# An add and GELU kernel: the first two loads of y take 16 KB and 48 KB per row instead of 32 KB each, into one buffer

## The chip, the cores and the metric

The kernel runs on one core of a Trainium2 chip. The metric is the device time of one execution in microseconds (us), lower is better. Before the change three executions took 120.02, 120.04 and 120.09 us, median 120.04.

## The reference

Two float32 matrices of 1024 x 4096 are added, and the GELU in its tanh form is taken of each element of the sum.

```python
z = x + y
return (0.5 * z * (1 + np.tanh(np.sqrt(2 / np.pi) * (z + 0.044715 * z ** 3)))).astype(np.float32)
```

16 MiB of x and 16 MiB of y are read and 16 MiB are written: 50.33 MB in all.

## The kernel before

Each of the 128 partitions holds eight rows of the matrix, which are 32,768 consecutive elements (128 KB) in memory. One tile z of that width holds x, then the sum, then the result, all in place. The work on it is cut into 16 chunks of 2,048 columns (`CH`). A chunk c passes through four steps:

- add c: z = z + y, on DVE for the chunks 0, 2, 4, 6, 8 and 12 (`by_dve`), on POOL for the other ten (line 149 for both).
- mag c: w = |z| on ACT, into a tile w in PSUM (line 154). There are two buffers of w (`PS = 2`), so mag c also needs end c-2.
- gelu c: w = gelu(-w) on ACT, in place (line 157).
- end c: z = max(z, 0) + w on DVE (line 166). This gives the GELU of z, since gelu(z) = max(z, 0) + gelu(-|z|). Chunk 8 (`FIRST`) does it in two halves.

All transfers are issued by SP, on one queue, in a fixed order: y0, x0, y1, x1, y2, y3, then the three stores. The loads of x have 16,384 columns each (64 KB per partition, 8 MiB), those of y 8,192 each (32 KB per partition, 4 MiB). "Row" below is what one transfer moves for one partition. y lies in a pool of two buffers of 8,192 columns, so y2 takes the buffer of y0 and has to wait for the adds of chunks 0 to 3, and y3 takes that of y1 and waits for the adds of chunks 4 to 7 (lines 129 to 132, and `needs` in lines 183 to 185). The stores have 16,384, 10,240 and 6,144 columns: chunks 0 to 7, 8 to 12 and 13 to 15. Each waits for the ends of its chunks, and store 0 also for the first half of end 8 (lines 137 to 143).

The order of each engine's instructions is written out by hand (lines 173 to 179). POOL takes its adds by rising chunk: 1, 3, 5, 7, 9, 10, 11, 13, 14, 15. ACT takes mag and gelu chunk by chunk. DVE takes add 0, add 2, end 0, end 1, add 4, end 2, end 3, add 6, end 4, end 5, end 6, end 7, add 8, end 8, end 9, add 12, end 10 and the ends after it. An engine works through its list strictly in order: an instruction that waits holds up all behind it. `begin_early` puts the issues of y0 and x0 ahead of the program's opening barrier; `wait_late` rearranges the closing waits. The change doesn't touch either.

Of the kernel before, what the change touches and what calls it, by code (L numbers as in the profile page):

```python
# [8 lines left out]
def begin_early(nc, count):  # L9


    head, body = (b.instructions for b in nc.main_func.blocks[:2])
    SP = mybir.EngineType.SP
    moved = [i for i in body if i.engine == SP and isinstance(i, mybir.InstDMACopy)][:count]
    assert not any(i.sync_info and i.sync_info.on_wait for i in moved)
    assert all(i.regs_accessed() == ((), ()) for i in moved)
    at = next(k for k, i in enumerate(head) if i.engine == SP)
    for k, i in enumerate(moved):
        body.remove(i)
        head.insert(at + k, i)  # L20


def wait_late(nc):

    body, end = (b.instructions for b in nc.main_func.blocks[1:3])
    last = [i for i in body if isinstance(i, mybir.InstDMACopy)][-1]
    (sem,) = [u.id for u in last.sync_info.on_update]
    all_done = end[0]  # L30
    reset = next(i for i in end if isinstance(i, mybir.InstDrain) and i.is_reset_sema)
    at = end.index(reset)
    clear = end[at + 1]
    first, stop = reset.reset_range_start, reset.reset_range_stop
    assert all_done.engine == mybir.EngineType.SP and reset.engine == mybir.EngineType.Pool
    assert isinstance(clear, mybir.InstISA) and clear.engine == mybir.EngineType.Pool
    waits = all_done.sync_info.on_wait
    (its,) = [w for w in waits if w.id == sem]

    end[0] = mybir.InstDrain(  # L40
        name=all_done.name, engine=all_done.engine, debug=all_done.debug, is_reset_sema=False,
        sync_info=mybir.SyncInfo(on_wait=[w for w in waits if w.id != sem], on_update=[]),
    )
    parts = []
    for f, e in ((first, sem), (sem + 1, stop)):
        if f < e:
            nc.gpsimd.sem_clear(range(f, e))
            parts.append(nc.cur_bb.bb.instructions.pop())
    end[at + 1 : at + 2] = parts
    end.append(  # L50
        mybir.InstEventSemaphore(
            name=clear.name, engine=mybir.EngineType.Activation, debug=clear.debug,
            sync_info=mybir.SyncInfo(
                on_wait=[its],
                on_update=[
                    mybir.SyncUpdate(
                        sync_type="semaphore", id=sem, ant_name=its.ant_name,
                        update_mode="sem-sub-imm", update_value=its.wait_value,
                    )
                ],  # L60
            ),
        )
    )


@with_exitstack
def kernel(
    ctx: ExitStack,
    tc: tile.TileContext,
    x: bass.AP,  # L70
    y: bass.AP,
    out: bass.AP,
):

    nc = tc.nc
    P = nc.NUM_PARTITIONS
    fp32 = mybir.dt.float32
    act = mybir.ActivationFunctionType
    alu = mybir.AluOpType

    N, D = x.shape
    assert N % P == 0
    TOT = N // P * D  # L90
    xv, yv, ov = (a.rearrange("(p n) d -> p (n d)", p=P) for a in (x, y, out))

    YS = 8192
    CH = 2048
    PS = 2
    xloads = [16384, 16384]
    yloads = [8192, 8192, 8192, 8192]
    FIRST = 8
    stores = [16384, 10240, 6144]

    def ranges(sizes):
        ends = [sum(sizes[: i + 1]) for i in range(len(sizes))]
        assert ends[-1] == TOT
        return [(e - f, e) for e, f in zip(ends, sizes)]

    xr, yr, sr, cr = (ranges(r) for r in (xloads, yloads, stores, [CH] * (TOT // CH)))
    C = len(cr)

    by_dve = {0: 0, 2: 0, 4: 2, 6: 4, 8: 8, 12: 10}

    def over(rs, lo, hi):
        return [i for i, (a, b) in enumerate(rs) if a < hi and b > lo]

    pool_sb = ctx.enter_context(tc.tile_pool(name="xz", bufs=1))
    pool_y = ctx.enter_context(tc.tile_pool(name="y", bufs=2))
    pool_w = ctx.enter_context(
        tc.tile_pool(name="w", bufs=PS, space=bass.MemoryType.PSUM)
    )

    zt = pool_sb.tile([P, TOT], fp32, tag="z", name="z")  # L120
    yt, wt, ends = {}, {}, {}

    def load_x(i):
        a, b = xr[i]
        nc.sync.dma_start(out=zt[:, a:b], in_=xv[:, a:b])

    def load_y(i):
        a, b = yr[i]
        s, o = divmod(a, YS)
        if o == 0:  # L130
            yt[s] = pool_y.tile([P, YS], fp32, tag="y", name=f"y{s}")
        nc.sync.dma_start(out=yt[s][:, o : o + b - a], in_=yv[:, a:b])  # L132

    def store(i):
        a, b = sr[i]
        ins = nc.sync.dma_start(out=ov[:, a:b], in_=zt[:, a:b])
        if i == 0:
            tc.add_manual_dep(
                ins.ins,
                ends[FIRST].name,  # L140
                mybir.DependencyInfo(mybir.DependencyClass.Sync, mybir.DependencyReason.DATA),
                reason="the stores join the queue when the last load is nearly done",
            )

    def add(c):
        a, b = cr[c]
        s, o = divmod(a, YS)
        eng = nc.vector if c in by_dve else nc.gpsimd
        eng.tensor_add(out=zt[:, a:b], in0=zt[:, a:b], in1=yt[s][:, o : o + b - a])  # L149

    def mag(c):
        a, b = cr[c]
        wt[c] = pool_w.tile([P, CH], fp32, tag="w", name=f"w{c}")
        nc.scalar.activation(out=wt[c], in_=zt[:, a:b], func=act.Abs)  # L154

    def gelu(c):
        nc.scalar.activation(  # L157
            out=wt[c], in_=wt[c], func=act.Gelu_apprx_tanh, scale=-1.0
        )

    def end(c):
        a, b = cr[c]
        parts = 2 if c == FIRST else 1
        n = (b - a) // parts
        for o in range(0, b - a, n):
            ins = nc.vector.scalar_tensor_tensor(  # L166
                out=zt[:, a + o : a + o + n], in0=zt[:, a + o : a + o + n], scalar=0.0,
                in1=wt[c][:, o : o + n], op0=alu.max, op1=alu.add,
            )
            ends.setdefault(c, ins.ins)  # L170


    sp = [(load_y, 0), (load_x, 0), (load_y, 1), (load_x, 1), (load_y, 2), (load_y, 3)]
    sp += [(store, i) for i in range(len(stores))]
    pool = [(add, c) for c in range(C) if c not in by_dve]
    dve, acts = [], []
    for c in range(C):
        dve += [(add, k) for k in sorted(by_dve) if by_dve[k] == c] + [(end, c)]
        acts += [(mag, c), (gelu, c)]

    needs = {
        load_x: lambda i: [],
        load_y: lambda i: [
            (add, c) for c in over(cr, yr[i][0] - 2 * YS, yr[i][1] - 2 * YS)
        ],
        add: lambda c: [(load_x, i) for i in over(xr, *cr[c])]
        + [(load_y, i) for i in over(yr, *cr[c])],
        mag: lambda c: [(add, c)] + ([(end, c - PS)] if c >= PS else []),
        gelu: lambda c: [(mag, c)],
        end: lambda c: [(gelu, c)],  # L190
        store: lambda i: [(end, c) for c in over(cr, *sr[i])] + [(end, FIRST)],
    }
    queues = [sp, pool, acts, dve]
    done = set()
    with tc.manual_schedule():
        one = pool_sb.tile([P, 1], fp32, tag="one", name="one")
        nc.vector.memset(one, 0.0)  # L197
        nc.scalar.activation(out=one, in_=one, func=act.Gelu_apprx_tanh)  # L198
        while any(queues):
            moved = False  # L200
            for q in queues:
                while q and all(n in done for n in needs[q[0][0]](q[0][1])):
                    fn, arg = q.pop(0)
                    fn(arg)
                    done.add((fn, arg))
                    moved = True
                    if q is not sp:
                        break
            assert moved, [q[:1] for q in queues]

    ctx.close()
    tc.close()
    tc.compile()  # L213
    begin_early(nc, 2)
    wait_late(nc)
# [30 lines left out]
```

## Time and profile before

| What | Value |
|---|---|
| Median of three executions | 120.04 us |
| The profiled execution | 120.05 us |
| Its span, from first to last record of the core | 118.6 us |
| Busy: DVE, ACT, POOL | 59.8, 60.8, 55.5 us |
| DMA queue, share of 16 engines | 98.6% |
| First adds start | 31.45 us (DVE), 31.49 us (POOL) |
| Stores issued | 77.61, 96.34 and 107.56 us |

DVE, ACT and POOL are compute engines; SP issues transfers. Times in the views count from the start of the span. Where a line of the profile starts with two numbers they are the start and the duration in us; then come the engine, the line of the kernel, the operation, what it writes and reads with its shape, and how many instructions are merged. What stands in square brackets is how long the engine had been idle before, and what ended that. "SPq" is SP's queue of instructions. "DMA to landing" is the time from a transfer's issue until its data has landed and been signalled.

### The profile page before, as it was taken

What the parts mean: (1) busy time and instruction counts of PE and PEld (TensorE: products, weight loads), DVE (VectorE), ACT (ScalarE), POOL (GpSimd) and SP (SyncE); (2) the same over time, 40 slices, a digit from 0 to 9 for tenths busy, and PEclk for the clock granted to TensorE, in tenths of its full rate; (3) what the DMA queues carried; (4) which work ended last, traced back from release to release, by engine and by line L of the source; (5) the groups of instructions that cost most, each with busy time, mean ns of one, the idle gap of its engine ahead of it and who ended that gap; (6) DMA issues with size and microseconds to landing.
All of it is one profiled execution on the core that took longest, in us unless ns stands there. A gap on an engine that the chain in (4) does not pass through costs nothing.

```text
span 118.6 us, 160 instructions
## 1 busy us (share of the span) xinstructions
DVE 59.8 (50%) x24; ACT 60.8 (51%) x34; POOL 55.5 (47%) x14
## 2 busy tenths in 40 slices
DVE  0000000000399999699994594257999457742000
ACT  5000000000067979999379705797798999940000
POOL 0000000000399999997000029999999999100000
DMA  7989888998889988988899898998899889999996
GB/s 243 464 365 696 354 354 354 663 398 354 354 387 497 531 354 354 707 354 354 354 420 464 365 520 354 531 531 354 354 531 531 354 354 442 442 442 442 398 398 265
DMA packets 1296, 50.33 MB, mean 424 GB/s; under 512 B 144, under 2 KB 144, under 8 KB 144
## 3 DMA queue, kind: packets, MB, share of 16 engines
q1 hardware_dynamic: 1296, 50.33, 98.6%
HBM read 33.55 MB, written 16.78 MB: 424 GB/s over the span
## 4 chain that ended last, share of the span: by engine, by line
DMA 48%; POOL 34%; POOLq 4%; ACT 3%; DVE 2%; issue 0%; SPq 0%; DVEq 0%
POOL z L149 34%; DMA z<-in_x_dram 26%; DMA y<-in_y_dram 21%; POOLq L213 4%; DVE z L166 2%; ACT w L154 2%; ACT w L157 2%; SPq L132 0%; POOLq L149 0%; DVEq L166 0%
## 5 line engine op out<-in xcount | busy, mean ns | idle before, releaser
L149 POOL TENSOR_TENSOR z<-z,y 128x2048 f32<-128x2048 f32 x10 | 55.3, 5563 | 45.6 <-DMA z<-in_x_dram 31.1
L154 ACT ACTIVATE w<-z 128x2048 f32<-128x2048 f32 x16 | 30.1, 1880 | 42.5 <-DVE z L149 36.0
L166 DVE SCALAR_TENSOR_TENSOR z<-z,w 128x2048 f32<-128x2048 f32 (+1 forms) x17 | 36.4, 2157 | 16.0 <-ACT w L157 16.0
L149 DVE TENSOR_TENSOR z<-z,y 128x2048 f32<-128x2048 f32 x6 | 24.0, 4009 | 30.3 <-DMA z<-in_x_dram 30.1
L157 ACT ACTIVATE w<-w 128x2048 f32<-128x2048 f32 x16 | 29.8, 1862 | 0.5
L198 ACT ACT_TABLE_LOAD x1 | 1.3, 1283 | 1.3 <-PEq L230 1.3
L197 DVE MEMSET one<- 128x1 f32 x1 | 0.1, 59 | 1.3 <-PEq L230 1.3
L198 ACT ACTIVATE one<-one 128x1 f32<-128x1 f32 x1 | 0.2, 203 | 0.0
L230 POOL MEMSET const-float32-0.0<- 128x1 f32 x1 | 0.1, 98 | 0.2 <-issue 0.2
L230 POOL MEMSET const-bfloat16-1.0<- 128x1 bf16 x1 | 0.1, 101 | 0.0
L230 POOL MEMSET const-uint8-127<- 128x1 uint8 x1 | 0.1, 101 | 0.0
L230 POOL MEMSET const-float32-1.0<- 128x1 f32 x1 | 0.1, 98 | 0.0
## 6 DMA issues: line engine op xcount, KB each, us to landing
y<-in_y_dram SPq DMA_DIRECT2D x4, 4096.0 KB, 23.7
out_dram<-z SPq DMA_DIRECT2D x1, 5120.0 KB, 14.9
out_dram<-z SPq DMA_DIRECT2D x1, 3072.0 KB, 11.0
z<-in_x_dram SPq DMA_DIRECT2D x2, 44.9
out_dram<-z SPq DMA_DIRECT2D x1, 21.6
```

Source lines behind the costliest of these rows:

```text
L149: eng.tensor_add(out=zt[:, a:b], in0=zt[:, a:b], in1=yt[s][:, o : o + b - a])
L154: nc.scalar.activation(out=wt[c], in_=zt[:, a:b], func=act.Abs)
L157: nc.scalar.activation(out=wt[c], in_=wt[c], func=act.Gelu_apprx_tanh, scale=-1.0)
L166: ins = nc.vector.scalar_tensor_tensor(out=zt[:, a + o : a + o + n], in0=zt[:, a + o : a + o + n], scalar=0.0, in1=wt[c][:, o : o + n], op ...
L197: nc.vector.memset(one, 0.0)
L198: nc.scalar.activation(out=one, in_=one, func=act.Gelu_apprx_tanh)
L213: tc.compile()
L230: nc = _bacc.Bacc("TRN2", target_bir_lowering=False, num_devices=1)
```

## The change

The two buffers of 8,192 columns become one tile of 16,384 columns, which takes as much memory. The first load of y brings 4,096 columns (16 KB per row, 2 MiB) and the second 12,288 (48 KB per row, 6 MiB); the third and fourth stay at 8,192. The order of SP's issues stays. A load of y goes to its column modulo 16,384, so y2 covers the columns of chunks 0 to 3 and y3 those of chunks 4 to 7.

```diff
-    YS = 8192
+    YS = 16384
     CH = 2048
     PS = 2
     xloads = [16384, 16384]
-    yloads = [8192, 8192, 8192, 8192]
+    yloads = [4096, 12288, 8192, 8192]
...
-    pool_y = ctx.enter_context(tc.tile_pool(name="y", bufs=2))
...
-    yt, wt, ends = {}, {}, {}
+    yt = pool_sb.tile([P, YS], fp32, tag="y", name="y")
+    wt, ends = {}, {}
...
     def load_y(i):
         a, b = yr[i]
-        s, o = divmod(a, YS)
-        if o == 0:
-            yt[s] = pool_y.tile([P, YS], fp32, tag="y", name=f"y{s}")
-        nc.sync.dma_start(out=yt[s][:, o : o + b - a], in_=yv[:, a:b])
+        o = a % YS
+        nc.sync.dma_start(out=yt[:, o : o + b - a], in_=yv[:, a:b])
...
-        s, o = divmod(a, YS)
+        o = a % YS
         eng = nc.vector if c in by_dve else nc.gpsimd
-        eng.tensor_add(out=zt[:, a:b], in0=zt[:, a:b], in1=yt[s][:, o : o + b - a])
+        eng.tensor_add(out=zt[:, a:b], in0=zt[:, a:b], in1=yt[:, o : o + b - a])
...
         load_y: lambda i: [
-            (add, c) for c in over(cr, yr[i][0] - 2 * YS, yr[i][1] - 2 * YS)
+            (add, c) for c in over(cr, yr[i][0] - YS, yr[i][1] - YS)
         ],
```

## The prediction

> **What bounds the kernel now.** I read the page's header and DMA rows first, then the time from issue to landing of each tile's transfers, then the instructions in order of time.
>
> ```profile
> span 118.6 us, 160 instructions
> DVE 59.8 (50%) x24; ACT 60.8 (51%) x34; POOL 55.5 (47%) x14
> q1 hardware_dynamic: 1296, 50.33, 98.6%
> ```
>
> No engine is busy for much over half of the span; the one DMA queue is busy for 98.6% of it. The two answers on tiles y and z give when each transfer landed:
>
> ```profile
> DMA to landing us min/median/max: 12.0/23.7/39.8
> DMA to landing us min/median/max: 11.0/21.6/58.8
> ```
>
> Added to the issue times (0.00, 0.43, 1.26, 1.64, 44.68, 57.94, 77.61, 96.34, 107.56) and with the page's row of issues, the landings are y0 12.0, x0 31.35, y1 41.06, x1 60.44, y2 70.14, y3 79.86, store 0 99.2, store 1 111.2, store 2 118.56. Their distances are 19.35 for 8 MiB, 9.71 for 4, 12.0 for 5 and 7.36 for 3: always 2.40 to 2.45 us per MiB, with rows from 24 to 64 KB. So the queue never runs dry, and the row size does not show. Only the first transfer is longer: 12.0 us for 4 MiB, of which 9.7 is stream and 2.3 is the time that a transfer on an idle queue costs beyond its stream (F below).
>
> The queue doesn't run dry because each issue comes early enough. SP's waits and issues:
>
> ```profile
> 44.68 0.33 SPq L132 DMA_DIRECT2D y<-in_y_dram  x1
> 57.94 0.33 SPq L132 DMA_DIRECT2D y<-in_y_dram  x1
> 77.61 0.35 SPq L136 DMA_DIRECT2D out_dram<-z  x1
> 96.34 0.34 SPq L136 DMA_DIRECT2D out_dram<-z  x1
> 107.56 0.33 SPq L136 DMA_DIRECT2D out_dram<-z  x1
> ```
>
> y2 is issued 15.8 us before x1 lands, y3 12.2 us before y2 lands. But store 0 is issued only 2.25 us before y3, the last load, lands; that is F itself, so this issue has next to no slack. Store 0 waits for the first half of end 8, which hangs on DVE's queue:
>
> ```profile
> 33.66 6.59 DVE L149 TENSOR_TENSOR z<-z,y 128x2048 f32<-128x2048 f32 x1
> 52.25 5.62 DVE L149 TENSOR_TENSOR z<-z,y 128x2048 f32<-128x2048 f32 x1
> 67.66 2.29 DVE L166 SCALAR_TENSOR_TENSOR z<-z,w 128x2048 f32<-128x2048 f32 x1 [1.46 <-ACT w L157]
> 70.23 2.29 DVE L149 TENSOR_TENSOR z<-z,y 128x2048 f32<-128x2048 f32 x1 [0.28 <-DMA y<-in_y_dram]
> 31.49 6.61 POOL L149 TENSOR_TENSOR z<-z,y 128x2048 f32<-128x2048 f32 x1 [31.06 <-DMA z<-in_x_dram]
> 51.21 4.51 POOL L149 TENSOR_TENSOR z<-z,y 128x2048 f32<-128x2048 f32 x1
> ```
>
> End 7 ran at 67.66 to 69.95, and add 8 started at 70.23 on the landing of y2: DVE's slack was 0.28 us. The lines also price the adds: 2.28 on DVE and 4.51 on POOL alone, 5.6 to 6.6 where they meet.
>
> **What the Trainium skill says.** "SBUF — State Buffer", in "Who interferes with whom": a DVE instruction with two SBUF inputs contends with a GpSimd instruction that reads SBUF, and the pair of ports is a lock held for the whole instruction. The trace agrees: POOL's add 1, started 0.04 us behind DVE's add 0, took 6.61 = 4.51 + 2.1, and DVE's add 6, started while POOL's add 7 ran (51.21 to 55.72), ended 2.15 after it, at 57.87. The end operation takes w from PSUM and took 2.27 to 2.29 beside POOL. "DMA: Bandwidth & Descriptors", in "Anatomy of one DMA — SWDGE (gpsimd) path", gives a fixed part of about 2.0 us per transfer; this is another path, but the 2.3 here is near it.
>
> **The change part by part.** In the program as built each engine keeps its order of instructions, and SP issues the same nine transfers; only sizes and waits differ.
>
> *Bytes and rows.* The sum of y0 and y1 stays 8 MiB, and each transfer has 128 rows. At 2.42 us per MiB, y1 still lands at 41.06, and x1, y2, y3 as before; only y0 and x0 land earlier, by 2 x 2.42 = 4.84. Cost 0. No row shows 16 or 48 KB; from 24 to 64 KB the price differs by at most 0.05 us per MiB, so for the 8 MiB the bounds are -0.4 and +0.4 us; I take 0.
>
> *Adds 2 and 3 wait for y1.* Before, chunks 0 to 3 were covered by y0. Now y0 holds chunks 0 and 1 alone. On DVE add 2 stands ahead of end 0 and of all behind it, on POOL add 3 ahead of adds 5 and 7. So DVE does add 0 alone, then stops until y1 has landed. I replay the queues with the rows' durations: DVE's next instruction starts 2.20 after the last, ACT's two take 1.88 and 1.86 with starts 1.91 and 1.77 apart (3.68 per chunk), an end starts 0.11 after its gelu, an add 0.09 after a landing.
>
> x0 lands at 31.35 - 4.84 = 26.51. Add 0 26.60 to 28.88, add 1 26.64 to 33.25, gelu 0 done 32.7, gelu 1 done 37.1. Then the wait for y1: add 2 41.16 to 43.44, add 3 on POOL 41.20 to 47.81 (behind add 2's lock). End 0 43.36 to 45.64, end 1 45.56 to 47.84. Add 4 47.76 to 50.04 and POOL's add 5 47.80 to 54.43. ACT: mag 2 needs end 0 (two w buffers): 45.68, gelu 2 done 49.45; gelu 3 51.27 to 53.13; mag 4 53.04, gelu 4 done 56.81; mag 5 56.72, gelu 5 done 60.49. End 2 49.96 to 52.24; end 3 53.24 to 55.53. Add 6 is asked for at 55.44, but POOL's add 7 has held the lock since 54.40, to 58.91; add 6 ends 2.15 later, at 61.06 (before: 57.87). End 4 60.99 to 63.26, end 5 63.19 to 65.46; mag 6 63.30, gelu 6 done 67.07; gelu 7 68.89 to 70.75; end 7 70.86 to 73.15, where it was 67.66 to 69.95: 3.2 us late.
>
> *Add 8 behind end 7.* It is asked for at 73.06. y2 landed at 70.14, and POOL's add 9, which before started 0.04 us behind add 8, starts at 70.27 and holds the lock to 74.78. So add 8 ends at 76.93 (before 72.52). Mag 8 76.97, gelu 8 done 80.74, first half of end 8 80.78 to 82.00; store 0 is issued at 82.02 instead of 77.61: 4.41 late.
>
> *The queue.* y3 lands at 79.86 as before. Store 0 lands F + 8 x 2.42 after its issue: 82.02 + 2.3 + 19.35 = 103.67 against 99.2, +4.47. F of a store on a queue run dry is not in the trace: from below, its issue of 0.35 and some 0.4 for the landing give 82.02 + 0.75 + 19.35 = 102.12, +2.9; from above the 2.3 of the first transfer, +4.5. With the skill's 2.0 it is +4.2. I take +4.3, between the last two.
>
> *Later stores.* DVE's add 12 is asked for at 86.7, behind POOL's add 13 (85.76 to 90.27), ends 92.4, and end 12 ends at 100.83 (before 96.31). Store 1 is issued at 100.86; it keeps the queue fed if this is before 82.02 + 19.35 = 101.37 (F on both sides cancels): 0.5 us of cover. Without it the excess would add to the end one to one. End 15 ends at 111.9, store 2 is due at 101.37 + 12.0 = 113.4: cover 1.5.
>
> *The refills.* y2 now waits for add 3 at 47.81: issued 47.9 (44.68), 10.2 us before it would be late at 60.44 - 2.3. y3 waits for add 6 at 61.06: issued 61.1, 6.7 before 70.14 - 2.3. Both cost 0 under the transfers ahead of them. One buffer in place of two adds no wait: y2's columns are those of adds 0 to 3, y3's of adds 4 to 7.
>
> Sum: span 118.6 + 4.3 = 122.9. This execution took 120.05 with 1.45 outside of the span (the median is 120.04): 124.35.
>
> **The rivals.** *No change, 120.05.* If DVE reached add 6 before POOL takes add 7 at 54.40, add 6 would end near 56.7, mag 6 would start at about 60.4 behind gelu 5, end 7 would end near 70.3, and add 8 would start on y2 as now. For it: chunks 0 and 1 leave ACT early, so only six of eight chunks (22 us) remain at 45.7. Against it: end 3 needs gelu 3 at 53.13, and end 3 would have to end by 54.4, not 55.5; the point from which this decides is 1.1 us.
>
> *The lock is given differently at add 8, 122.7.* If add 8 ran at once at 73.06, it would end at 75.3, and store 0 would be issued at 80.4, 2.8 late, which with the F taken above is +2.65 at the end. Against it: add 6 and add 2 each waited out a whole POOL add.
>
> *Add 8 misses POOL's gap at 74.78, 128.8.* If it were asked for 1.7 us later than worked out, add 10 would hold the lock until 79.3, and all is 4.5 later. Were add 4 to lose the lock to add 5 at 47.8 (they are 0.04 apart), add 6 still ends near 61.2 and add 8 is asked for at about 73.9: inside the gap.
>
> *Faster.* The load path would have to shrink, and no byte leaves it; the 0.4 us bound on rows, with no late store, would be 119.6.
>
> **How the numbers follow.** Forecast 0.81; no change 0.06; lock given at once 0.05; missed gap 0.06; faster 0.02. The forecast's own range is 122.9 to 125.2: F's lower bound (118.6 + 2.9 + 1.45 = 122.95) to F 2.3 with 0.4 for rows or a late store 1. To leave out no more than two in ten the range takes in the lock given at once: 122.6 to 125.4. About 0.2% is what a measurement of this kernel can tell from no change. Slower: 0.81 + 0.05 + 0.06 = 0.92; same 0.06; faster 0.02.
>
> **What would show it.** x0 lands near 26.5 and y1 still near 41; add 2 waits for y; end 7 ends near 73; add 8 takes well over 2.3 us; store 0 is issued near 82, and the DMA row falls in the slices at 80 to 84; the waits of ACT for DVE grow. It is wrong if add 6 ends before 58.5, if store 0 is issued before 78, or if the transfers' pace moves from 2.42 us per MiB.

## The result and the profile after

The changed kernel takes 123.82 us (median of six, 123.76 to 123.90) against 120.11 for the kernel before, measured beside it: a ratio of 1.0309, 95% interval 1.0296 to 1.0323. It is slower by 3.7 us. The forecast was 124.35, in a range of 122.6 to 125.4.

The page of the changed kernel, its header and the rows on DMA (the row of digits is the DMA engines' busy share in 40 slices of 3.06 us):

```profile
span 122.4 us, 161 instructions
DVE 57.8 (47%) x24; ACT 60.4 (49%) x34; POOL 55.5 (45%) x14
DMA  7999779859959897799789897709777979999596
q1 hardware_dynamic: 1296, 50.33, 95.8%
```

The span grew by 3.8 us and no engine is busy for longer; the queue's share fell from 98.6% to 95.8%. The place is the one 0 in the row of digits, the 27th slice, 79.6 to 82.6 us: the queue stood still there. From 79.5 to 82.9 us it moved nothing at all. A table by stretch of time (columns: the stretch, its length, busy time of DVE, ACT and POOL with instructions, clock, share of the DMA engines, GB/s) shows it beside the same stretch of the kernel before; first the changed kernel:

```profile
79.90:83.00 3.10, 2.10 (x2) 3.07 (x3) 3.10 (x2) 1.00 0.05 21
```

and the kernel before:

```profile
79.90:83.00 3.10, 2.20 (x1) 2.40 (x2) 3.10 (x2) 1.00 0.78 338
```

(In so short a stretch the share of the DMA engines is coarse: for 70.0 to 79.9 us the same table gives the kernel before a share of 1.10.)

What ended the gap is SP's issue of store 0. SP's issues in the changed kernel, in order of time (start, duration):

```profile
47.96 0.33 SPq L131 DMA_DIRECT2D y<-in_y_dram  x1
61.22 0.33 SPq L131 DMA_DIRECT2D y<-in_y_dram  x1
82.15 0.35 SPq L135 DMA_DIRECT2D out_dram<-z  x1
100.86 0.34 SPq L135 DMA_DIRECT2D out_dram<-z  x1
111.98 0.33 SPq L135 DMA_DIRECT2D out_dram<-z  x1
```

y2 and y3 are issued 3.3 us later than before, still long ahead of need. Store 0 is issued at 82.15 instead of 77.61, 4.54 us late, after y3 has landed (at about 80.0). The way to it, on DVE and POOL:

```profile
26.79 2.29 DVE L148 TENSOR_TENSOR z<-z,y 128x2048 f32<-128x2048 f32 x1 [25.39 <-DMA z<-in_x_dram]
41.24 2.29 DVE L148 TENSOR_TENSOR z<-z,y 128x2048 f32<-128x2048 f32 x1 [12.16 <-DMA y<-in_y_dram]
47.85 2.29 DVE L148 TENSOR_TENSOR z<-z,y 128x2048 f32<-128x2048 f32 x1
55.53 5.60 DVE L148 TENSOR_TENSOR z<-z,y 128x2048 f32<-128x2048 f32 x1
54.47 4.51 POOL L148 TENSOR_TENSOR z<-z,y 128x2048 f32<-128x2048 f32 x1
70.92 2.29 DVE L165 SCALAR_TENSOR_TENSOR z<-z,w 128x2048 f32<-128x2048 f32 x1 [1.46 <-ACT w L156]
73.13 3.93 DVE L148 TENSOR_TENSOR z<-z,y 128x2048 f32<-128x2048 f32 x1
70.41 4.51 POOL L148 TENSOR_TENSOR z<-z,y 128x2048 f32<-128x2048 f32 x1 [11.42 <-DMA y<-in_y_dram]
```

and add 4 in the kernel before:

```profile
44.57 2.28 DVE L149 TENSOR_TENSOR z<-z,y 128x2048 f32<-128x2048 f32 x1
```

From the top: add 0 starts 4.7 us earlier than before. Add 2 then keeps DVE idle for 12.16 us until y1 has landed, although gelu 0 is done at 32.89 and end 0 could run. Add 4 starts at 47.85, 3.28 us later than before, and this delay is handed on: add 6 is asked for at 55.53 (before 52.25), waits out POOL's add 7 (54.47 to 58.98) and ends at 61.13; end 7 ends at 73.21. Waiting out add 7 is not new: in the kernel before add 6 came behind add 7 by nearly as much (52.25 against 51.21), so it adds nothing to the loss. What is newly lost is the turn at the shared ports that add 8 had ahead of add 9. DVE had 0.28 us to spare there, so add 8 is asked for 2.9 us later than before; POOL's add 9 (70.41 to 74.92) has started by then, add 8 waits it out and takes 1.64 us longer. It ends at 77.06, 4.54 us later than before.

### The profile page after: what moved, and what is told of

Its sections match the earlier page's. It is cut to its first block, busy times and chain, and to the rows that moved or that the text cites. A ratio compares the mean times of both kernels' runs of the same rounds, so it can differ in the third digit from the quotient of the medians.

```text
span 122.4 us, 161 instructions
## 1 busy us (share of the span) xinstructions
DVE 57.8 (47%) x24; ACT 60.4 (49%) x34; POOL 55.5 (45%) x14
## 3 DMA queue, kind: packets, MB, share of 16 engines
q1 hardware_dynamic: 1296, 50.33, 95.8%
## 4 chain that ended last, share of the span: by engine, by line
DMA 33%; ACT 29%; DVE 15%; issue 14%; DVEq 0%
DMA y<-in_y_dram 33%; ACT w L153 18%; ACT w L156 10%; DVE z L165 8%; DVE z L148 7%; DVEq L165 0%
## 5 line engine op out<-in xcount | busy, mean ns | idle before, releaser
L148 DVE TENSOR_TENSOR z<-z,y 128x2048 f32<-128x2048 f32 x6 | 22.1, 3676 | 37.6 <-DMA z<-in_x_dram 25.4
## 6 DMA issues: line engine op xcount, KB each, us to landing
out_dram<-z SPq DMA_DIRECT2D x1, 5120.0 KB, 14.2
out_dram<-z SPq DMA_DIRECT2D x1, 20.8
```

What stands on the lines that cost most here:

```text
L148: eng.tensor_add(out=zt[:, a:b], in0=zt[:, a:b], in1=yt[:, o : o + b - a])
```

## The experiments

The theory, Q: the two loads of y themselves cost nothing. Adds 2 and 3 wait for y1, and add 2 stands at the head of DVE's queue; DVE's and POOL's adds shut each other out; so end 7 and with it end 8 are late, and store 0 is issued only after the queue has run dry. The rivals: R, the rows of 16 and 48 KB or the shared tile cost the time; S, store 0 is the only transfer that is late.

**The shared tile alone.**

```diff
-    yloads = [4096, 12288, 8192, 8192]
+    yloads = [8192, 8192, 8192, 8192]
```

> The one tile for y is kept, but all four loads of y have 8,192 columns (32 KB rows) again. If the loss is store 0 coming late because chunks 2 and 3 wait for y1, nothing is late here: add 2 starts at about 33.7 us, store 0 is issued at 77.6 and the time is 120.1. If the shared tile itself cost something (an added wait of y2 or y3), the time stays near 123.8.

Measured: 120.07 us, ratio to before 1.0002 (0.9991 to 1.0013). One tile in place of two buffers costs nothing; the sizes of the loads are the part that matters.

**A smaller step in the sizes.**

```diff
-    yloads = [4096, 12288, 8192, 8192]
+    yloads = [6144, 10240, 8192, 8192]
```

> In one tile, y0 has 6,144 columns and y1 10,240, so y0 covers chunks 0 to 2 and only add 3, on POOL, waits for y1. By the queues: add 2 is done near 38, ends 0 and 1 before 43, end 7 ends near 67.4, before y2 lands at 70.1, so store 0 is issued near 77.6 and the time is 120.1: a step, not a slope. If unequal rows cost in proportion, about 121.9.

Measured: 120.05 us, ratio 0.9993 (0.9982 to 1.0003). Half of the change costs nothing, so the loss is a step and not in proportion to the rows. Here y0 covers chunks 0 to 2, so that add 2 does not wait for y1. Add 3 on POOL still does; then come end 7 and add 8 of this run:

```profile
41.07 17.63 POOL L148 TENSOR_TENSOR z<-z,y 128x2048 f32<-128x2048 f32 x3 [5.44 <-DMA y<-in_y_dram]
64.88 2.29 DVE L165 SCALAR_TENSOR_TENSOR z<-z,w 128x2048 f32<-128x2048 f32 x1 [1.46 <-ACT w L156]
70.17 2.29 DVE L148 TENSOR_TENSOR z<-z,y 128x2048 f32<-128x2048 f32 x1 [3.01 <-DMA y<-in_y_dram]
```

POOL's wait for y1 alone costs nothing. DVE is done with end 7 at 67.17 and waits 3.01 us for y2: slack where the kernel before had 0.28 us and the changed kernel none.

**Add 2 moved behind end 1, rows of 16 and 48 KB kept.**

```diff
-    by_dve = {0: 0, 2: 0, 4: 2, 6: 4, 8: 8, 12: 10}
+    by_dve = {0: 0, 2: 2, 4: 2, 6: 4, 8: 8, 12: 10}
```

> The changed kernel with one move: on DVE add 2 stands behind end 1 instead of ahead of end 0. If the loss comes from add 2 heading DVE's queue while y1 is on its way, ends 0 and 1 now run before 40 us, add 6 gets the port before add 7, end 7 ends near 69.5, store 0 is issued near 77.6, and the time is 120.1 with rows of 16 and 48 KB. If the rows or the tile cost the time, it stays at 123.8.

Measured: 120.02 us, ratio 0.9992 (0.9979 to 1.0006). DVE and POOL around y1 and at add 6:

```profile
37.08 2.29 DVE L165 SCALAR_TENSOR_TENSOR z<-z,w 128x2048 f32<-128x2048 f32 x1 [2.14 <-ACT w L156]
54.09 2.28 DVE L148 TENSOR_TENSOR z<-z,y 128x2048 f32<-128x2048 f32 x1
54.12 6.63 POOL L148 TENSOR_TENSOR z<-z,y 128x2048 f32<-128x2048 f32 x1
66.92 2.29 DVE L165 SCALAR_TENSOR_TENSOR z<-z,w 128x2048 f32<-128x2048 f32 x1 [1.47 <-ACT w L156]
```

The first line is end 1, done before y1 lands. Add 6 now comes 0.03 us ahead of POOL's add 7, runs in 2.28 us, and it is POOL that waits: the turn that the changed kernel and the kernel before both lost. End 7 ends at 69.21, in time for y2. The loads are those of the changed kernel, so R falls: the place of one instruction in DVE's queue decides over the whole loss.

**A late store 0 alone, on the kernel before.**

```diff
-    FIRST = 8
+    FIRST = 9
```

Store 0 now waits for the first half of end 9 in place of end 8.

> The kernel before, with the loads as they were; FIRST is 9 instead of 8, so store 0 waits for the first half of end 9 and is issued near 82.05 instead of 77.61. If a late store 0 alone is enough, the queue runs dry as in the changed kernel: store 0 lands 20.8 after its issue, at 102.85 instead of 99.2, and the time is 123.7. If the loss is in the loads or the compute, it is 120.1.

Measured: 123.82 us, ratio 1.0307 (1.0282 to 1.0331), the changed kernel's time with the old loads. The issue and, from the page's DMA issues, its time to landing:

```profile
82.01 0.35 SPq L136 DMA_DIRECT2D out_dram<-z  x1
out_dram<-z SPq DMA_DIRECT2D x1, 20.8
```

Stores 1 and 2 are issued at 96.33 and 107.52, as in the kernel before, so here nothing else is late. A store 0 issued at 82 is enough for the whole loss.

**Store 0 freed of end 8, in the changed kernel.** The manual dependence of store 0 is left out, and

```diff
-        store: lambda i: [(end, c) for c in over(cr, *sr[i])] + [(end, FIRST)],
+        store: lambda i: [(end, c) for c in over(cr, *sr[i])],
```

> The changed kernel, but store 0 waits only for the ends of its own chunks 0 to 7 and is issued near 73.2, before y3 lands. If store 0's lateness is the whole loss: 120.1. If all of the later chunks are late with it, store 1 (chunks 8 to 12, 100.86) comes after store 0 has landed at 99.2; it lands 14.2 after its issue at 115.1, store 2 7.4 later at 122.4, and the time is 123.8 as before this edit.

Measured: 123.15 us, ratio 1.0241 (1.0211 to 1.0271). S falls: with store 0 issued at 73.11, 3.0 us of the loss stay, 2.0 of them now ahead of store 1.

```profile
100.75 0.34 SPq L135 DMA_DIRECT2D out_dram<-z  x1
out_dram<-z SPq DMA_DIRECT2D x1, 5120.0 KB, 13.6
out_dram<-z SPq DMA_DIRECT2D x1, 27.1
```

The last line is store 0: it lands at 73.11 + 27.1 = 100.2, 0.5 us before store 1 is issued; store 1 lands at 114.35 and store 2 about 7.3 later. Store 1 took 1.5 us more than the 12.1 that its 5 MiB take in a busy queue at 2.42 us each, so to leave no gap it had to be issued at about 98.7; it came about 2.0 us after that. The expected 123.8 was 0.65 too much because it took for store 1 the 14.2 us of the changed kernel, where it had stood in the queue; on an empty queue it took 13.6. And store 0 ought to have landed at 99.2, not 100.2. That is the other 1.0 us; more on it below.

**Smaller stores, with store 0 waiting as in the change.**

```diff
-    stores = [16384, 10240, 6144]
+    stores = [16384, 4096, 4096, 4096, 4096]
```

> The changed kernel with stores of 16,384 and four times 4,096 columns; store 0 still waits for the first half of end 8. The later stores are then ready well ahead, but store 0 comes at 82.15: the queue has 1.5 us of fixed part and 38.7 us of stream behind that, so about 122.4 of span and 123.8 if the dry queue before store 0 is the loss; 120.1 if the lateness of store 1 or 2 is.

Measured: 124.01 us, ratio 1.0313 (1.0287 to 1.0338). Smaller later stores, the first of them issued at 86.94 in place of 100.86, gain nothing while store 0 is late.

**Both: store 0 freed, and smaller stores.**

> Both edits: store 0 freed of end 8 (issued near 73.2) and four later stores of 4,096 columns. The compute ends as late as in the changed kernel (end 15 near 112), but each store is issued before the queue has worked off the one ahead: ends 9, 11, 13, 15 near 87, 97, 105, 112 against 97.8, 102.6, 107.5, 112.3. Then 120.1. If the late compute itself sets the end: 112 + 1.5 + 4.9 is 118.4 of span, the same; if more stores cost on the queue, or if rows of 16 and 48 KB do, over 121.

Measured: 121.21 us, ratio 1.0079 (1.0055 to 1.0104). Most of the loss is gone, though the compute ends as late as in the changed kernel: the last two stores are issued at 104.57 and 111.93. But 1.1 us stays where nothing was expected to. The queue shows no gap, at 98.8% of a span of 119.8. Store 0 was issued at 73.16 and took 27.1 to land, so at 100.26; less its stream of 19.35 that puts the landing of y3 at 80.9, 1.0 later than in the kernel before. This was new. Store 0 freed alone, without smaller stores, had lost the same 1.0, so the smaller stores were the least likely cause; the store's early issue and the rows were open.

**Store 0 freed in the kernel before**, with the same edit on the old loads and stores.

> The kernel before, loads untouched; store 0 waits only for the ends of chunks 0 to 7 and is issued near 70.0 instead of 77.6, long before y3 has landed. If a store queued behind a running load slows that load, as in the two runs with store 0 freed (y3 landed at 80.85 and 80.89 instead of 79.86), y3 lands near 80.9 here too and the time is 121.1. If the extra 1.0 us there came from the new rows or the smaller stores, it is 120.1.

Measured: 121.24 us, ratio 1.0078 (1.0053 to 1.0103). The page and SP's line:

```profile
69.94 0.35 SPq L136 DMA_DIRECT2D out_dram<-z  x1
out_dram<-z SPq DMA_DIRECT2D x1, 30.4
q1 hardware_dynamic: 1296, 50.33, 98.7%
```

69.94 + 30.4 - 19.35 = 81.0: y3 lands 1.1 late again, with neither new rows nor small stores. It is the early issue. That it is the load which takes longer, and not the store, is read from y3 alone, issued at 57.94 in the kernel before and at 57.90 here; its time to landing there and here:

```profile
DMA to landing us min/median/max: 21.9/21.9/21.9
DMA to landing us min/median/max: 23.1/23.1/23.1
```

**Smaller stores, and store 0 waiting for add 8.** Store 0's manual dependence names add 8 in place of the first half of end 8, and the stores are 16,384 and four times 4,096.

> The changed kernel with stores of 16,384 and four times 4,096 columns, and store 0 waiting for add 8 instead of end 8: issued near 77.1, neither late nor long ahead. If the whole loss is the dry queue, and the 1.1 us left with store 0 freed came from its early issue, y3 lands at 79.9, the queue never runs dry and the time is 120.1, with rows of 16 and 48 KB and all compute from chunk 2 to 15 as late as in the changed kernel. If smaller stores cost the rest, 121.2.

Measured: 120.25 us, ratio 0.9998 (0.9980 to 1.0016).

```profile
76.86 0.35 SPq L135 DMA_DIRECT2D out_dram<-z  x1
111.76 0.33 SPq L135 DMA_DIRECT2D out_dram<-z  x1
q1 hardware_dynamic: 1584, 50.33, 98.8%
```

The span is 118.5. Rows of 16 and 48 KB, the shared tile, the late adds and a compute that ends near 112 are all still there and cost nothing, since store 0 comes neither after y3 nor long ahead of it and each later store in time. None of the versions is faster than the kernel before: where the queue never runs dry and store 0 is not issued long ahead of y3's landing, the span is 118.5 or 118.6.

## Why the prediction was right

**Bytes and rows: 0.** Right. y1 was due to land at 41.06 and add 2 started on it at 41.24; y2, due at 70.14, started add 9 at 70.41. The runs with loads of y in rows of 16, 24, 40 and 48 KB whose store 0 is neither late nor freed of its wait are at 120.0 to 120.3.

**Adds 2 and 3 and the replay of the queues.** Right to about 0.2 us in every step shown here: x0 in use at 26.79 (26.60 forecast), add 6 asked for at 55.53 (55.44) and ended at 61.13 (61.06), end 7 ended at 73.21 (73.15). Moving add 2 showed that its place at the head of the queue is the cause. The rival of no change was said to decide at add 6's turn at the port, which add 6 lost by 1.06 us (55.53 against 54.47); with add 2 moved it won the turn, and that rival came true. The turn is what a repair can win back and not where the loss arose, since add 6 had lost it in the kernel before as well.

**Add 8 behind end 7.** Right: asked for at 73.13 (73.06), ended at 77.06 (76.93). The rival in which the port is given at once is out. The lock that the Trainium skill describes in "SBUF — State Buffer", "Who interferes with whom", is seen in all runs: the second add waits out the whole of the first. A waiting add on DVE ended 2.15 to 2.21 us after POOL's, one on POOL 4.35 to 4.40 after DVE's.

**The queue: +4.3.** The direction and the mechanism were right, the size was 0.5 too large, and the term mis-sized is F, the time beyond the stream that a transfer on a dry queue takes. I took it between the 2.3 of the first load and the 2.0 that the Trainium skill gives in "DMA: Bandwidth & Descriptors", "Anatomy of one DMA — SWDGE (gpsimd) path", for transfers issued on another path. Store 0 took 20.8 from issue to landing here and in the run with FIRST at 9; less 19.35 of stream F is 1.45. The measurement decides: neither the page's figure for the other path nor the first load stands for a store on a dry queue. The lower bound of 0.75 was too small; the trace has 0.85 us from the issue to the store's first packet alone. So the latest issue without a gap in the kernel before was 99.2 - 20.8 = 78.4, and its slack was 0.8 us, where I had put next to none. The sum is then 4.54 late less 0.8 of slack, 3.74; the span grew by 3.8 and the time by 3.71. F alone would have put the forecast 0.7 too high; that store 0 came 4.54 late and not 4.41 took 0.1 of it back.

**Later stores and refills: 0.** Right. Store 1 was issued at 100.86, as forecast, before store 0 landed at 82.15 + 20.8 = 102.95. That it has little cover (0.5 us forecast) is what store 0 freed alone ran into: once store 0 no longer holds the queue up, store 1 is the next one late.

## What to carry to other kernels

Here one queue was busy for 98% of the span, and to start the first add almost 5 us earlier gained nothing, even where nothing else came late (120.02 with add 2 moved). In such a kernel ask of each transfer how much earlier it is issued than the queue would run dry, and what its issue hangs on. Splitting loads so that the first part lands sooner moves other columns into a later load: what chunks 2 and 3 waited for last was x0 (31.35) before the change and y1 (41.2) after it. In an engine's strict order an instruction that waits for such a load holds up work that is ready; moving that instruction behind the ready work gave back all of the loss. A stall that is repaired at one store may only move to the next: repaired at the stores, the loss went away only when the first store's wait and the size of the later ones changed together.

## What was not expected

A store that was issued long before the last load had landed slowed that load. With store 0 issued at 69.94, 73.11 and 73.16, y3 landed at about 80.9 to 81.0; with store 0 issued at 76.86, 77.61 and 82.15 it landed by 80.0, and the difference of 1.0 to 1.1 us stays in the time (121.24 and 121.21 against 120.25 and 120.1). Between y3 and store 0 the queue shows no gap in these three runs. So the issue of store 0 has a window: its start lies between 73.2 and 76.9, and its end is near 78.4 by the slack worked out above.

The traces' records of single packets, one row each, show where the load slows. Each of the 16 DMA engines moves eight rows of y3. With store 0 freed, the last 32 rows, two for each engine, took up to 2.32 to 2.39 us in the three runs, in place of the 1.21 to 1.22 of the kernel before. No row ahead of them took more than 1.26, although store 0 was issued while they were under way. Why the last two rows slow was not tried and stays open.

The second point is F: 1.45 us for a store on an empty queue, 2.3 for the first load of the program. A part of the difference shows in the same records: in the kernel before, the first row on the DMA engines took up to 2.14 us where rows of that size took 1.21 later on, while the first rows of store 0 on the dry queue took at most 2.47 us against 2.42 later on.
